# A dilated convolution's last stores: part of them issued by GpSimd, spread anew over the DMA engines

## The chip, the core and the metric

The kernel runs on one core of one Trainium2 chip. The metric is the device time of one launch in microseconds (us); lower is better. Each time is compared with the kernel before as it is printed below.

## What is computed

A 3x3 convolution with dilation 2 and "same" padding: 16 images of 64 channels and 64x64 points, 128 output channels, all in float32 in HBM.

```python
batch, c_in, h, w, c_out, k, dilation = 16, 64, 64, 64, 128, 3, 2
x_pad = np.pad(x, ((0, 0), (0, 0), (4 // 2, 4 // 2), (4 // 2, 4 // 2)))
for b, co, ci, kh, kw:
    output[b, co] += weight[co, ci, kh, kw] * x_pad[b, ci, kh*2:kh*2+h, kw*2:kw*2+w]
```

The input is 16.8 MB, the output 33.6 MB, the weights 0.3 MB.

## The kernel before

**Tiling.** Two images make a pair: 2 x 64 channels fill the 128 partitions, so a pair's input is one tile `x32` of 128 x 4096 float32. There are 8 pairs (`pb`, 0 to 7). A pair's 64 rows are worked on in 4 groups of 16 rows (`g`), so the main loop (L200) runs over G = 0 to 31, with pb = G // 4 and g = G % 4. For each group ScalarE casts input rows to float16 (L74), VectorE adds pairs of rows (L86), TensorE makes three products (`psA`, `psB`, `psP`, all L172), ScalarE copies `psP` to `p_sb` (L234), and VectorE adds `p_sb` to `psA` and to `psB` (L241), which gives the even and the odd pairs of output rows. The two adds write the group's rows into the pair's output tile `osb`: 128 partitions (output channels) x 2 images x 4096 points in float32. Three `osb` tiles are in use in turn.

**Order.** The program is scheduled by hand (`tc.manual_schedule()`, L57): every engine runs its instructions in the order in which they are written, and the framework adds only the waits. All DMAs, loads and stores alike, are issued by SyncE (SP) on one queue. Their completions are told on eight semaphores used in turn, so each DMA of SP waits, before it is issued, until the one eight places ahead of it has landed, besides waiting for the data that it needs. GpSimd (POOL) works only in the first 5.2 us of the program: constants, an identity matrix, and two of the weight transforms (L113, L116).

**How a DMA is cut.** A row of a partition that is contiguous on both sides is one packet. A store of 32 rows of one image over 128 partitions is 128 packets of 8 KB (32 x 64 x 4 bytes); over 16 DMA engines that is 8 packets for each. Each share of a DMA ends with a packet of 4 bytes, which tells the semaphore.

**Stores.** From the fourth pair on (`pb` 3 to 6) a pair is stored when it is finished, one image at a time (L276, L277, 2 MB each). The last pair (`pb` 7, G = 28 to 31) is stored in halves of 32 rows: after G = 29 rows 0 to 32 of image 0 (L269), rows 0 to 24 of image 1 (L271), and rows 24 to 32 of image 1 in two DMAs, one over partitions 0 to 124 and one over partitions 124 to 128 (`FOUR`, L197, L272; `ROWS4 = 8`, L198). After G = 31 rows 32 to 64 of both images follow (L269, L274). The function `store` (L184) makes a DMA of one image, `store_both` (L191) one of both images.

Of the kernel before, what the change touches and what calls it, by code (L numbers as in the profile page):

```python
# [10 lines left out]
def kernel(  # L11
# [7 lines left out]
    nc = tc.nc  # L19

    B, CI, H, W = x.shape
# [7 lines left out]
    P = 128  # L29
    f32 = mybir.dt.float32  # L30
# [5 lines left out]
    GR = 16  # L36
    NG = H // GR
# [7 lines left out]
    wpool = ctx.enter_context(tc.tile_pool(name="wpool", bufs=1))  # L45
# [8 lines left out]
    x_pair = x.rearrange("(nb two) c h w -> nb (two c) (h w)", two=2)  # L54
    out_img = out.rearrange("b o h w -> b o (h w)")
# [3 lines left out]
    x32_tiles, x16_tiles, xs_tiles, o_tiles = {}, {}, {}, {}  # L59

    def load(pb, cuts=(0, H)):
        if pb not in x32_tiles:
            x32_tiles[pb] = fpool.tile([P, HW], f32, tag="x32", name="x32")
        for lo, hi in zip(cuts[:-1], cuts[1:]):
            nc.sync.dma_start(  # L65
                out=x32_tiles[pb][:, lo * W : hi * W], in_=x_pair[pb, :, lo * W : hi * W]
            )
# [10 lines left out]
    def rowsum(c):  # L78
        pb, g = divmod(c, NG)
        if g == 0:  # L80
            xs_tiles[pb] = sxpool.tile([P, HW // 2], f16, tag="xs", name="xs")
        v = x16_tiles[pb][:, g * GR * W : (g + 1) * GR * W].rearrange(
            "p (b e q) -> p b e q", e=2, q=2 * W
        )
        s = xs_tiles[pb][:, g * NH : (g + 1) * NH].rearrange("p (b q) -> p b q", q=2 * W)
        nc.vector.tensor_tensor(out=s, in0=v[:, :, 0], in1=v[:, :, 1], op=add)  # L86
# [27 lines left out]
    nc.scalar.copy(out=wdv[:, 2], in_=wv[:, 0])  # L114
    nc.vector.tensor_tensor(out=wdv[:, 1], in0=wv[:, 2], in1=wv[:, 1], op=sub)
    nc.gpsimd.tensor_copy(out=wdv[:, 4], in_=wv[:, 2])  # L116

    wts = [apool.tile([P, 1024], f32, tag="ab", name="wt") for _ in range(3)]

    def turn(k):  # L120
# [24 lines left out]
        out=x16_tiles[0][:, 8 * W : 18 * W], in_=x32_tiles[0][:, 8 * W : 18 * W]  # L145
# [8 lines left out]
    def casts(G):  # L154
        for n in range(2 if G else 3):
            c = ahead[0]
            if c >= ngroups or c > G + (7 if c < 2 * NG else 5):
                return
            cast(c)
            ahead[0] += 1  # L160

    def product(ps, src, kind, blk0, nblk, first, last):
        for j in (1, 0, 2):
            dw = (j - 1) * d
            o0, o1 = max(0, -dw), W - max(0, dw)
            t = kind * KW + j
            for hb in range(2):
                pp = slice(hb * CI, (hb + 1) * CI)
                rhs = src(pp, dw + o0, dw + o1)
                po = ps[:, hb * NH + blk0 * 2 * W : hb * NH + (blk0 + nblk) * 2 * W]  # L170
                po = po.rearrange("p (r w) -> p r w", w=W)[:, :, o0:o1]
                nc.tensor.matmul(  # L172
                    out=po,
                    lhsT=w_sb[pp, t * CO : (t + 1) * CO],
                    rhs=rhs,
                    start=first and j == 1,
                    stop=last and j == 2,
                )

    def blocks(x16, b0, n, e):  # L180
        v = x16.rearrange("p (b e r w) -> p b e r w", e=2, r=2, w=W)
        return lambda pp, c0, c1: v[pp, b0 : b0 + n, e, :, c0:c1]

    def store(pb, m, r0=0, r1=H, rows=((0, P),)):  # L184
        for lo, hi in rows:
            nc.sync.dma_start(
                out=out_img[2 * pb + m, lo:hi, r0 * W : r1 * W],
                in_=o_tiles[pb][lo:hi, m * HW + r0 * W : m * HW + r1 * W],
            )

    def store_both(pb, r0, r1):  # L191
        nc.sync.dma_start(
            out=out_img[2 * pb : 2 * pb + 2, :, r0 * W : r1 * W].rearrange("m o q -> o m q"),
            in_=o_tiles[pb].rearrange("p (m q) -> p m q", m=2)[:, :, r0 * W : r1 * W],
        )

    FOUR = ((0, P - 4), (P - 4, P))  # L197
    ROWS4 = 8  # L198

    for G in range(ngroups):  # L200
        pb, g = divmod(G, NG)
        x16 = x16_tiles[pb]
        xs = xs_tiles[pb].rearrange("p (r w) -> p r w", w=W)
        if g == 0:
            o_tiles[pb] = opool.tile([P, 2 * HW], f32, tag="osb", name="osb")
        o = o_tiles[pb].rearrange("p (m b e q) -> p m b e q", m=2, e=2, q=2 * W)
        b0 = g * NBLK

        def summed():
            ps = ppool.tile([P, 2 * NH], f32, tag="p", name="psP")  # L210
            sv = lambda pp, c0, c1: xs[pp, g * GR // 2 : (g + 1) * GR // 2, c0:c1]
            product(ps, sv, 0, 0, NBLK, True, True)
            return ps

        if G:
            psP = summed()

        psA = apool.tile([P, 2 * NH], f32, tag="ab", name="psA")
        product(psA, blocks(x16, b0, NBLK, 1), 1, 0, NBLK, True, False)
        z = 1 if g == 0 else 0  # L220
        product(psA, blocks(x16, b0 + z - 1, NBLK - z, 1), 2, z, NBLK - z, False, True)

        psB = apool.tile([P, 2 * NH], f32, tag="ab", name="psB")
        product(psB, blocks(x16, b0, NBLK, 0), 3, 0, NBLK, True, False)
        z = 1 if g == NG - 1 else 0
        product(psB, blocks(x16, b0 + 1, NBLK - z, 0), 4, 0, NBLK - z, False, True)

        if not G:
            psP = summed()

        if not G:
            casts(0)
        p_sb = spool.tile([P, 2 * NH], f32, tag="psb", name="p_sb")
        nc.scalar.copy(out=p_sb, in_=psP)  # L234
        if G:
            casts(G)
        if G + 1 < ngroups:
            rowsum(G + 1)
        pv = p_sb.rearrange("p (m b q) -> p m b q", m=2, q=2 * W)
        for e, ps in ((0, psA), (1, psB)):  # L240
            nc.vector.tensor_tensor(  # L241
                out=o[:, :, b0 : b0 + NBLK, e],
                in0=ps.rearrange("p (m b q) -> p m b q", m=2, q=2 * W),
                in1=pv,
                op=add,
            )

        if G == 0:
            load(XF, (0, H // 2))
        if pb == 0:  # L250
            if g % 2 == 1:
                store_both(0, (g - 1) * GR, (g + 1) * GR)
                if g == 1:
                    load(XF, (H // 2, H))
                else:
                    load(XF + 1)
        elif g == NG - 1 and pb == 1:
            store(1, 0)
            store(1, 1, 0, H // 2)
            load(XF + 2)  # L260
            store(1, 1, H // 2, H)
        elif g == NG - 1 and pb == 2:
            store(2, 0)
            load(XF + 3)
            store(2, 1)
            load(XF + 4)
        elif pb == npairs - 1:
            if g % 2 == 1:
                store(pb, 0, (g - 1) * GR, (g + 1) * GR)  # L269
                if g == 1:  # L270
                    store(pb, 1, 0, 2 * GR - ROWS4)  # L271
                    store(pb, 1, 2 * GR - ROWS4, 2 * GR, FOUR)  # L272
                else:
                    store(pb, 1, (g - 1) * GR, (g + 1) * GR)  # L274
        elif g == NG - 1:
            store(pb, 0)  # L276
            store(pb, 1)  # L277
# [37 lines left out]
```

## Time and profile before

| | us |
|---|---|
| time, median of 3 runs | 126.88 |
| the three runs | 126.70, 127.41, 126.88 |
| span of the profiled execution, first to last instruction | 125.0 |
| what the median has beyond that span | 1.9 |
| busy in the span: TensorE / VectorE / ScalarE / GpSimd | 105.8 / 91.0 / 64.9 / 2.2 |
| time of the SP queue's packets, as a share of 16 DMA engines' span | 96.7% |

The execution that was profiled has no time of its own in the list of runs; its span stands 1.9 us below their median, and this is taken as what lies around it.

How to read it: the page gives each engine's busy time, then the span in 40 slices of 3.1 us (a digit is the busy share in tenths), the DMA queues, and the DMA issues by size. A view by stretches of time gives, for each stretch, the share of the 16 DMA engines' time that packets took (1.00 is all 16 busy; packets are counted where they start, so a stretch can read a little over 1) and the rate in GB/s. The trace also holds every DMA packet with its start, duration and size, but not the number of the engine that moved it. On one engine the packets follow each other without a gap, the next one starting 3 ns before the recorded end of the last, so the records can be joined to 16 chains, one for each engine; where such chains are spoken of below, they were joined in this way.

### The profile page before, as it was taken

What the parts mean: (1) busy time and instruction counts of PE and PEld (TensorE: products, weight loads), DVE (VectorE), ACT (ScalarE), POOL (GpSimd) and SP (SyncE); (2) the same over time, 40 slices, a digit from 0 to 9 for tenths busy, and PEclk for the clock granted to TensorE, in tenths of its full rate; (3) what the DMA queues carried; (4) which work ended last, traced back from release to release, by engine and by line L of the source; (5) the groups of instructions that cost most, each with busy time, mean ns of one, the idle gap of its engine ahead of it and who ended that gap; (6) DMA issues with size and microseconds to landing.
All of it is one profiled execution on the core that took longest, in us unless ns stands there. A gap on an engine that the chain in (4) does not pass through costs nothing.

```text
span 125.0 us, 2343 instructions
## 1 busy us (share of the span) xinstructions
PE 105.8 (85%) x1002; PEld 57.0 (46%) x1002; DVE 91.0 (73%) x103; ACT 64.9 (52%) x68; POOL 2.2 (2%) x8
## 2 busy tenths in 40 slices
PE   6996999999999999999999999999999999600000
PEld 2353555555555555555555555555555555200000
DVE  0561998988898889888988898889888988700000
ACT  4188896665666566656665666566653333100000
POOL 2400000000000000000000000000000000000000
PEclk9999999999999999999999999999999999985555
DMA  5999999999999999999999999999999999999991
GB/s 142 368 450 435 430 401 315 430 422 420 443 427 435 412 441 438 401 435 435 425 430 427 420 435 430 435 420 435 420 430 430 430 425 435 430 414 412 420 395 73
DMA packets 4722, 50.78 MB, mean 406 GB/s; under 512 B 488, under 2 KB 488, under 8 KB 1000
## 3 DMA queue, kind: packets, MB, share of 16 engines
q1 hardware_dynamic: 4712, 50.63, 96.7%
q8 instruction: 8, 0.13, 0.4%
q14 instruction: 2, 0.02, 0.0%
HBM read 17.07 MB, written 33.55 MB: 405 GB/s over the span
## 4 chain that ended last, share of the span: by engine, by line
PE 76%; DMA 6%; ACT 2%; DVE 1%; DVEq 1%; SPq 1%; issue 0%
PE psA L172 31%; PE psB L172 30%; PE psP L172 16%; DMA x<-in_x_dram 6%; ACT x L74 2%; DVE osb L241 1%; DVEq L310 1%; ACT p_sb L234 1%; SPq L65 0%; SPq L89 0%; DVEq L241 0%
## 5 line engine op out<-in xcount | busy, mean ns | idle before, releaser
L172 PEld LDWEIGHTS <-w_sb 64*128 64x128 f16 x960 | 54.6, 94 | 45.8 <-issue 1.4
L234 ACT COPY p_sb<-psP 128x1024 f32<-128x1024 f32 x32 | 32.4, 1012 | 36.9 <-issue 21.5
L241 DVE TENSOR_TENSOR osb<-psA,p_sb 128x1024 f32<-128x1024 f32 x32 | 39.2, 1225 | 13.4 <-PE psA L172 9.8
L172 PE MATMUL psA<-x,w_sb 64*128 64x496 f16 (+3 forms) x384 | 45.1, 365 | 0.0
L172 PE MATMUL psB<-x,w_sb 64*128 64x496 f16 (+3 forms) x384 | 45.1, 365 | 0.0
L241 DVE TENSOR_TENSOR osb<-psB,p_sb 128x1024 f32<-128x1024 f32 x32 | 39.1, 1222 | 0.0
L74 ACT CAST x<-x 128x1024 f16<-128x1024 f32 (+2 forms) x31 | 32.1, 1044 | 0.5 <-DMA x<-in_x_dram 0.3
L172 PE MATMUL psP<-xs,w_sb 64*128 64x496 f16 (+1 forms) x192 | 26.0, 371 | 1.1 <-ACT p_sb L234 1.1
L86 DVE TENSOR_TENSOR xs<-x 128x512 f16<-128x512 f16 x32 | 13.3, 416 | 0.4 <-ACT x L74 0.4
L102 PE MATMUL dm<-zero 128*128 128x512 f16 x12 | 5.3, 579 | 1.2 <-DVE zero L94 1.2
L102 PEld LDWEIGHTS <-zero 128*128 128x128 f16 x12 | 1.4, 128 | 3.2 <-issue 1.8
L112 DVE CAST wd<-w 128x192 f16<-128x192 f32 x1 | 0.5, 503 | 2.4 <-DMA w<-in_weight_dram 2.4
L125 PEld LDWEIGHTS <-wd 128*64 128x64 f16 x30 | 1.0, 118 | 1.8 <-DVE wd L112 0.8
L137 ACT CAST w_sb<-wt 128x384 f16<-128x384 f32 x1 | 0.5, 478 | 2.3 <-PE wt L125 2.3
L114 ACT ACT_TABLE_LOAD x1 | 1.3, 1283 | 0.7 <-PEq L296 0.7
L125 PE MATMUL wt<-ident,wd 128*64 128x128 f16 x30 | 1.6, 241 | 0.0
L114 ACT CAST wd<-w 128x192 f16<-128x192 f32 x1 | 0.5, 539 | 1.5 <-DMA w<-in_weight_dram 1.5
L139 DVE CAST w_sb<-wt 128x384 f16<-128x384 f32 x1 | 0.6, 557 | 0.7 <-PE wt L125 0.7
L135 DVE CAST w_sb<-wt 128x384 f16<-128x384 f32 x1 | 0.6, 558 | 0.5 <-PE wt L125 0.5
L94 DVE MEMSET zero<- 128x256 uint32 x1 | 0.3, 272 | 0.9 <-PEq L296 0.9
L113 POOL TENSOR_TENSOR wd<-w 128x192 f16<-128x192 f32 x1 | 0.8, 799 | 2.3 <-DMA w<-in_weight_dram 2.3
L116 POOL CAST wd<-w 128x192 f16<-128x192 f32 x1 | 0.8, 806 | 0.0
(11 smaller groups left out, 3.8 us busy)
## 6 DMA issues: line engine op xcount, KB each, us to landing
out_dram<-osb SPq DMA_DIRECT2D x13, 2048.0 KB, 14.9
x<-in_x_dram SPq DMA_DIRECT2D x6, 2048.0 KB, 17.0
out_dram<-osb SPq DMA_DIRECT2D x5, 1024.0 KB, 13.1
x<-in_x_dram SPq DMA_DIRECT2D x2, 1024.0 KB, 13.2
x<-in_x_dram SPq DMA_DIRECT2D x1, 1088.0 KB, 5.6
x<-in_x_dram SPq DMA_DIRECT2D x1, 960.0 KB, 7.4
out_dram<-osb SPq DMA_DIRECT2D x1, 768.0 KB, 15.4
w<-in_weight_dram SPq DMA_DIRECT2D x1, 288.0 KB, 2.8
```

Of the source, the lines that this page charges most:

```text
L74: nc.scalar.copy(out=x16_tiles[pb][:, lo * W : hi * W], in_=x32_tiles[pb][:, lo * W : hi * W])
L86: nc.vector.tensor_tensor(out=s, in0=v[:, :, 0], in1=v[:, :, 1], op=add)
L102: nc.tensor.matmul(out=dm[:, 0:512], lhsT=zero[:, 0:P], rhs=zero)
L113: nc.gpsimd.tensor_tensor(out=wdv[:, 3], in0=wv[:, 0], in1=wv[:, 1], op=sub)
L114: nc.scalar.copy(out=wdv[:, 2], in_=wv[:, 0])
L116: nc.gpsimd.tensor_copy(out=wdv[:, 4], in_=wv[:, 2])
L125: nc.tensor.matmul(out=wts[k % 3][r * CI : (r + 1) * CI, c0 + j * CO : c0 + (j + 1) * CO], lhsT=wd[:, t * CI : (t + 1) * CI], rhs=ident,)
L135: nc.vector.tensor_copy(out=t0[0], in_=t0[1])
L172: nc.tensor.matmul(out=po, lhsT=w_sb[pp, t * CO : (t + 1) * CO], rhs=rhs, start=first and j == 1, stop=last and j == 2,)
L234: nc.scalar.copy(out=p_sb, in_=psP)
L241: nc.vector.tensor_tensor(out=o[:, :, b0 : b0 + NBLK, e], in0=ps.rearrange("p (m b q) -> p m b q", m=2, q=2 * W), in1=pv, op=add,)
L310: with _tile.TileContext(nc) as tc:
```

## The change

Three things are changed.

- After the weight transforms GpSimd issues a small load: 5 partitions, two pieces of 16 numbers each, into a new tile `step` that nothing reads.
- After G = 28 GpSimd stores rows 0 to 8 of both images of the last pair over partitions 0 to 121 (`ELEVEN` = 11 x 11), in one DMA with two pieces for each partition. What is left of these rows (partitions 121 to 125, and 125 to 128) is stored by SP after G = 29 in two small DMAs.
- After G = 29 the other stores start at row 8: rows 8 to 32 of image 0, rows 8 to 28 of image 1, and rows 28 to 32 of image 1 in the two DMAs of `FOUR` (`ROWS4` is 4 instead of 8). The stores after G = 31 are the same.

```diff
     nc.gpsimd.tensor_copy(out=wdv[:, 4], in_=wv[:, 2])
+    step = wpool.tile([5, 32], f32, name="step")
+    nc.gpsimd.dma_start(
+        out=step.rearrange("p (s n) -> p s n", s=2),
+        in_=x_pair[0, 0:5, 0 : 2 * W].rearrange("p (s n) -> p s n", s=2)[:, :, 0:16],
+    )
...
-    def store_both(pb, r0, r1):
-        nc.sync.dma_start(
-            out=out_img[2 * pb : 2 * pb + 2, :, r0 * W : r1 * W].rearrange("m o q -> o m q"),
-            in_=o_tiles[pb].rearrange("p (m q) -> p m q", m=2)[:, :, r0 * W : r1 * W],
+    def store_both(pb, r0, r1, lo=0, hi=P, eng=nc.sync):
+        both = out_img[2 * pb : 2 * pb + 2, lo:hi, r0 * W : r1 * W]
+        eng.dma_start(
+            out=both.rearrange("m o q -> o m q"),
+            in_=o_tiles[pb].rearrange("p (m q) -> p m q", m=2)[lo:hi, :, r0 * W : r1 * W],
         )
 
     FOUR = ((0, P - 4), (P - 4, P))
-    ROWS4 = 8
+    ROWS4 = 4
+    ELEVEN = 11 * 11
+    ROWS11 = 8
...
         elif pb == npairs - 1:
-            if g % 2 == 1:
+            if g == 0:
+                store_both(pb, 0, ROWS11, 0, ELEVEN, nc.gpsimd)
+            elif g == 1:
+                store(pb, 0, ROWS11, 2 * GR)
+                store(pb, 1, ROWS11, 2 * GR - ROWS4)
+                store(pb, 1, 2 * GR - ROWS4, 2 * GR, FOUR)
+                store_both(pb, 0, ROWS11, ELEVEN, ELEVEN + 4)
+                store_both(pb, 0, ROWS11, ELEVEN + 4, P)
+            elif g == NG - 1:
                 store(pb, 0, (g - 1) * GR, (g + 1) * GR)
-                if g == 1:
-                    store(pb, 1, 0, 2 * GR - ROWS4)
-                    store(pb, 1, 2 * GR - ROWS4, 2 * GR, FOUR)
-                else:
-                    store(pb, 1, (g - 1) * GR, (g + 1) * GR)
+                store(pb, 1, (g - 1) * GR, (g + 1) * GR)
```

## The prediction, made before the changed kernel ran

> **What bounds the kernel now.** I read the page's slices and queue rows first, to see which resource is full.
>
> ```profile
> DMA  5999999999999999999999999999999999999991
> GB/s 142 368 450 435 430 401 315 430 422 420 443 427 435 412 441 438 401 435 435 425 430 427 420 435 430 435 420 435 420 430 430 430 425 435 430 414 412 420 395 73
> ...
> q1 hardware_dynamic: 4712, 50.63, 96.7%
> ```
>
> The DMA engines are full from the second slice to the last but one, all on SP's queue. So the time is the bytes of each of 16 engines at that engine's rate, and the end is that of the engine that ends last. TensorE and VectorE matter only if a store comes so late that an engine runs dry. The VectorE rows in order of time show when the last groups are written; the waits of SP show what the program's end waits for.
>
> ```profile
> 98.79 1.22 DVE L241 TENSOR_TENSOR osb<-psB,p_sb 128x1024 f32<-128x1024 f32 x1
> ...
> 101.96 1.22 DVE L241 TENSOR_TENSOR osb<-psB,p_sb 128x1024 f32<-128x1024 f32 x1
> ...
> 108.25 1.22 DVE L241 TENSOR_TENSOR osb<-psB,p_sb 128x1024 f32<-128x1024 f32 x1
> ```
>
> ```profile
> SPq L310 <- DMA out_dram<-osb: 13.2, 3, 8.5
> ```
>
> G = 28 is written at 100.0 us, G = 29 at 103.2, G = 31 at 109.5; then nothing but stores runs for 15 us. What counts is how evenly the engines end. The view by stretches shows it:
>
> ```profile
> 119.00:120.00 1.00, 0.00 (x0) 0.00 (x0) 0.00 (x0) 0.00 (x0) 0.00 (x0) 0.50 1.03 434
> 120.00:120.50 0.50, 0.00 (x0) 0.00 (x0) 0.00 (x0) 0.00 (x0) 0.00 (x0) 0.50 0.97 410
> ...
> 121.50:122.00 0.50, 0.00 (x0) 0.00 (x0) 0.00 (x0) 0.00 (x0) 0.00 (x0) 0.50 0.74 311
> 122.00:122.50 0.50, 0.00 (x0) 0.00 (x0) 0.00 (x0) 0.00 (x0) 0.00 (x0) 0.50 0.35 147
> 122.50:123.00 0.50, 0.00 (x0) 0.00 (x0) 0.00 (x0) 0.00 (x0) 0.00 (x0) 0.50 0.31 131
> 123.00:123.50 0.50, 0.00 (x0) 0.00 (x0) 0.00 (x0) 0.00 (x0) 0.00 (x0) 0.50 0.20 82
> 123.50:124.00 0.50, 0.00 (x0) 0.00 (x0) 0.00 (x0) 0.00 (x0) 0.00 (x0) 0.50 0.04 16
> ```
>
> The last column but one, times 16, is the number of busy engines: all until 120.5, about 6 at 122.25, 3 at 123.25. The chains of packets say which. The 2 KB packets of the two `FOUR` stores are on four engines only, 31 + 1 on each; I call these the low four. They end at 122.91, 123.49, 123.68 and 123.81. The twelve others end at 120.35, 120.61, 120.91, eight from 121.73 to 122.61, and one at 123.45. That one is slow: from about 30 us to 108 us its 16 KB packets mostly take some 644 ns, where the others' take 611. So five engines end within 0.9 us, and the mean of all 16 ends is 122.26, which only a perfect spread would reach (1.55 us earlier).
>
> Beside the numbers of engines: 124 rows went to 4 engines, 128 rows go to 16, so an SP transfer is cut into the largest number of equal shares up to 16 that divides its rows.
>
> **The change, part by part.** Packet prices from the chains, start to start: 8 KB 306 ns, 6 KB 230, 2 KB 80 (84 recorded). A line through 80 and 306 gives 193 for 5 KB and 42 for 1 KB.
>
> 1. Rows 0 to 8 leave the two wide stores after G = 29. Every engine saves 8 x (306 - 230) = 0.61 us on image 0. On image 1 the wide part shrinks from 24 to 20 rows: 8 x (230 - 193) = 0.30. Together -0.91 on all 16.
>
> 2. `FOUR` with half the rows: on the low four 32 x 80 = 2.56 becomes 32 x 42 = 1.34. The two small SP stores (4 and 3 rows, two pieces of 2 KB) put 2 x 80 = 0.16 each on the low four and on three of them. Net for the low four: -0.91 - 2.56 + 1.34 + 0.32 = -1.81 (-1.97 for one). They end at 122.0 at the latest and no longer set the end.
>
> 3. The GpSimd store: 121 rows. By the same division that is 11 engines with 11 rows, 22 packets of 2 KB. No row shows a packet of GpSimd's queue. From below, the nearest row is SP's 2 KB store packet, 80 ns; nothing makes it cheaper, since the bytes are the same. From above, I take the only second queue in the trace, the instruction fetch of 16 KB: it cost its engine 1.33 us where a data packet costs 0.607, 2.2 times, so 176 ns. I take 84, the recorded duration without the overlap of 3 to 4 ns, because it is the same kind of transfer (SBUF to HBM, 2 KB) and packets of two queues need not overlap. So 22 x 84 = 1.85, and with part 1 +0.94 on eleven engines (up to 22 x 176 = 3.87, +2.96).
>
> 4. Which eleven? The load over 5 rows goes ahead of the store, on 5 engines. If GpSimd's transfers go round the engines from the lowest, the store lies on numbers 5 to 15, and number 4 gets only part 1, -0.91. The trace doesn't number the twelve; I assume that the slow one is one of the eleven, which by count alone is 11 in 12. It then ends at 123.45 + 0.94 = 124.39, against 123.81 now: **+0.58**. The next is 122.61 + 0.94 = 123.55.
>
> By the Trainium skill ("DMA: Bandwidth & Descriptors", "Latency and other measured facts") engines 7 and 15 are usually the slow ones, which it ties to descriptor rings of GpSimd's path. The trace agrees that one engine is slow (644 ns against 611), though before the change no DMA is on that path, so the reason given can't be this one. By that rule the slow engine has a number from 5 to 15 and the sum is the one above; without it the count 11 in 12 stands.
>
> 5. The small load: 10 packets of 64 bytes at about 6 us, on five engines. They can't cost more than the weight load's 2304-byte packets (mostly 93 ns): two for each engine, under 0.2 us on engines that don't end last. On GpSimd it comes behind its last transform (ends at 5.1 us), with nothing after it until G = 28. Zero.
>
> 6. Issue and waits. GpSimd waits for VectorE's G = 28 (100.0 us) and then writes the descriptors. The data are wanted by about 117 us only, since each engine has SP's stores queued until then: zero unless that takes over 10 us. SP issues six DMAs after G = 29 instead of four, 0.73 us each, from 103.2 to 107.6, ahead of G = 31 (109.5): zero. But the last pair now has eight SP DMAs instead of six, so by the turn of eight semaphores the two last stores wait for the two stores of pair 6, which landed at 109.86 and 114.73, plus what GpSimd's packets push them back (up to 1.85). The first may be issued at up to 111.5 instead of 109.5, the second at about 116.6 instead of 109.9. With 0.7 us of issue and 0.6 to the first packet (the weight load: issued 0.74, first packet 1.76) the second is there at 117.9. The first low engine that wants it ends its share of the first at 122.91 - 1.81 - 2.45 = 118.65. So 0.75 us of cover: zero. If the cover went (176 ns per packet: landing at 118.6, packets at 119.9) the low four would idle 1.25 us and end by 123.2, still not last.
>
> 7. The program's end waits for each semaphore in turn. Now the last store's is the last; after the change it comes earlier in that row, and GpSimd's two are added. I put 0.15 us, two or three passed waits at the 0.06 us between the last waits of the trace; bounds 0 and 0.4.
>
> Sum: +0.58 + 0.15 = +0.73. Against the profiled execution: 125.0 + 0.7 = 125.7 us of span; with the 1.9 between this span and the median of 126.88: **127.6 us**.
>
> **Rivals.**
>
> *The slow engine is the spared one (number 4).* Not slower. It then gains 0.91 and ends at 122.54; the end is the next of the eleven, 123.55, -0.26 against 123.81, with 0.15 for the waits 126.8. It decides as soon as the engine at 123.45 is outside the eleven. If in the timed runs it lags more than here, the time before is later by as much and the time after isn't: 1.0 us of further lag gives 125.8. For it: it is the only engine that the change relieves relative to the eleven, and the trace has no numbers. Against it: one in twelve by count.
>
> *GpSimd's packets cost more.* At 176 ns the slow engine ends at 123.45 + 2.96 = 126.4, +2.6, with the waits 129.6; halfway, at 130 ns, 128.6. For it: the fetch rows, where a switch between queues cost about 0.7 us beyond the packet itself. Against it: a fetch isn't a store from SBUF.
>
> *The eleven are other engines, or sixteen.* If the store starts at the lowest engine as SP's do, the low four get 1.85 as well and end at 123.81 - 1.81 + 1.85 = 123.85: 127.1 if the slow engine isn't hit, 127.6 if it is. If the rows go to 16 engines, 8 rows each, an engine takes 16 x 84 = 1.34 and nets +0.43: the slow one ends at 123.88, 127.1; were it the one with a single row left, 126.5. For the last the skill (same page, "Why a DMA increments its semaphore by 16 and not by 1") knows a spread by 16 for some GpSimd copies and going round in turn for the others; no row here shows either.
>
> **How the numbers follow.** Forecast (slow engine among the eleven, packets of 80 to 100 ns, waits 0 to 0.4: 127.3 to 128.2): 0.40. Slow engine spared (125.8 to 127.0): 0.30; more than the count gives, because the twelve aren't numbered and the same time comes out if that engine is slow only while it is recorded. Dearer packets (128.2 to 129.6): 0.20. Other engines (126.5 to 127.6): 0.10. The bound for a change is 0.5%, 0.63 us, about what separates the three runs. Over 127.5: 0.30 of the forecast and all of the dearer packets, 0.50. Under 126.25: 0.17 of the spared, 0.03 of the last. The rest 0.30. The range 126.1 to 129.2 leaves out some 0.10 below and 0.08 above; the forecast's own is 127.3 to 128.2.
>
> **What would show it.** A second data queue with 252 data packets; 22 packets of 2 KB from it on each of eleven chains, at about 84 ns; the low four ending about 122; a share of 16 engines that stays near 1 until 121.2 and a single engine left after 123.6. I am wrong if the last engine is one of the many, or if all engines idle before the last store.

## The result, and the profile after

The changed kernel takes 128.80 us (median of four runs, 128.55 to 129.13) against 126.88 for the three runs of the kernel before; the ratio is 1.0155, with a 95% interval of 1.0114 to 1.0196. A fourth run of before (130.27) was disturbed and isn't in the ratio. The forecast was 127.6, with a range of 126.1 to 129.2. The profiled execution took 129.13, with a span of 127.3, so 1.85 us lie around it.

The lines below are from the page of the changed kernel: the slices and the queues.

```profile
DMA  4999999999999999999999999999999999999970
GB/s 130 380 458 438 417 404 366 440 391 422 448 438 422 404 456 389 435 420 427 438 420 422 417 427 433 438 407 443 422 438 417 433 427 404 415 383 367 385 296 41
...
q1 hardware_dynamic: 4733, 50.13, 94.9%
q0 software_dynamic: 224, 0.50, 1.0%
```

Still no empty slice before the end, and the second queue (q0, GpSimd's) has only 0.50 MB. Its 224 packets are, for the store, 121 of 4 KB, 55 of 8 bytes and 16 of 4 bytes, and for the load 5 of 128 bytes, 11 of 8 and 16 of 4. So the 4 KB packets lie on 11 engines, 11 on each, and every engine outside gets 8-byte packets in their place, 11 on each of five; I call these padding. But the slices 36 to 38 carry 383, 367 and 385 GB/s, where the kernel before had 414, 412 and 420: the engines are busy and move less. The view by stretches of the same kernel shows where (the last two columns are the DMA share and the rate):

```profile
104.00:106.00 2.00, 2.00 (x23) 1.01 (x19) 1.62 (x2) 0.10 (x1) 0.00 (x0) 1.00 0.95 403
106.00:108.00 2.00, 2.00 (x22) 1.11 (x20) 1.25 (x2) 1.01 (x1) 0.00 (x0) 1.00 0.98 393
108.00:110.00 2.00, 0.56 (x8) 0.13 (x3) 1.91 (x2) 0.00 (x0) 0.00 (x0) 1.00 1.05 418
110.00:112.00 2.00, 0.00 (x0) 0.00 (x0) 0.00 (x0) 0.00 (x0) 0.00 (x0) 1.00 0.99 397
...
116.00:118.00 2.00, 0.00 (x0) 0.00 (x0) 0.00 (x0) 0.00 (x0) 0.00 (x0) 0.50 0.99 313
118.00:119.00 1.00, 0.00 (x0) 0.00 (x0) 0.00 (x0) 0.00 (x0) 0.00 (x0) 0.50 0.95 339
...
124.00:125.00 1.00, 0.00 (x0) 0.00 (x0) 0.00 (x0) 0.00 (x0) 0.00 (x0) 0.50 0.25 107
```

The same stretches of the kernel before, which the prediction didn't show:

```profile
104.00:106.00 2.00, 2.00 (x24) 1.05 (x20) 2.00 (x2) 0.19 (x1) 0.00 (x0) 1.00 1.03 442
106.00:108.00 2.00, 2.00 (x22) 1.00 (x18) 1.25 (x2) 0.82 (x1) 0.00 (x0) 1.00 0.99 418
108.00:110.00 2.00, 0.11 (x2) 0.00 (x0) 1.46 (x2) 0.00 (x0) 0.00 (x0) 1.00 1.05 442
110.00:112.00 2.00, 0.00 (x0) 0.00 (x0) 0.00 (x0) 0.00 (x0) 0.00 (x0) 0.92 0.91 389
...
116.00:118.00 2.00, 0.00 (x0) 0.00 (x0) 0.00 (x0) 0.00 (x0) 0.00 (x0) 0.50 1.03 426
118.00:119.00 1.00, 0.00 (x0) 0.00 (x0) 0.00 (x0) 0.00 (x0) 0.00 (x0) 0.50 1.05 436
...
124.00:125.00 1.00, 0.00 (x0) 0.00 (x0) 0.00 (x0) 0.00 (x0) 0.00 (x0) 0.50 0.00 0
```

Two stretches lose bytes while the share stays near 1. From 116 to 119 us the kernel before moves 2 x 426 + 436 = 1288 KB, the changed one 2 x 313 + 339 = 965. At some 27 KB per us and engine (16 KB in 0.607 us), 323 KB over 16 engines are 0.75 us of every engine. From 104 to 112 us it is 3382 against 3222 KB, 0.37 us. A share near 1 with a low rate means packets that take longer than their size. The packet records say the same. Take for every packet its recorded time beyond the normal one of its size (611 ns for 16 KB, 309 for 8 KB, 234, 196, 159, 84 and 46 for 6, 5, 4, 2 and 1 KB); from 97 us on this sums to 0.08 us per engine before and to 1.08 after. I call it stall. There are two bursts: 16 KB packets, from 106 to 112 us, while GpSimd's store runs; and the small and 8 KB packets after that, mostly from 116 to 119 us, when GpSimd's store has landed (112.5 to 114.9 us).

SP's queue and the waits, in the changed kernel (first the DMA issues in order of time: start, duration; then waits: total, times, longest):

```profile
103.66 6.16 SPq L191 DMA_DIRECT2D out_dram<-osb  x4
109.87 3.15 SPq L198 DMA_DIRECT2D out_dram<-osb  x2
113.11 4.68 SPq L191 DMA_DIRECT2D out_dram<-osb  x2
```

```profile
SPq L322 <- DMA out_dram<-osb: 8.3, 1, 8.3
...
SPq L191 <- DMA out_dram<-osb: 3.3, 1, 3.3
```

Before, four issues after G = 29 took 0.33, 0.64, 0.73 and 0.73 us. Now six take 0.33, 1.66, 1.97, 2.05, 1.68 and 1.42, so the first store of G = 31 is issued at 113.11 instead of 109.49. The last is issued at 117.44, after the wait of 3.3 us for the landing of a store of pair 6 (117.43). VectorE is only 0.45 us later than before (the last writes of G = 28, 29 and 31):

```profile
99.24 1.23 DVE L249 TENSOR_TENSOR osb<-psB,p_sb 128x1024 f32<-128x1024 f32 x1
...
102.41 1.23 DVE L249 TENSOR_TENSOR osb<-psB,p_sb 128x1024 f32<-128x1024 f32 x1
...
108.69 1.21 DVE L249 TENSOR_TENSOR osb<-psB,p_sb 128x1024 f32<-128x1024 f32 x1
```

Where the 2.3 us of span went can be read from the landings, 16 for each wide store. I measure from the mean landing of the store of pair 5's second image (issued at about 85 us, ahead of everything that the GpSimd store touches; 102.97 before, 103.09 after) to the mean landing of the last store, and call this the drain.

| | before | after | difference |
|---|---|---|---|
| mean landing of pair 5's second image | 102.97 | 103.09 | +0.12 |
| from there to the mean landing of the last store (drain) | 19.64 | 20.87 | +1.23 |
| from that mean to the last landing | 1.53 | 2.12 | +0.59 |
| from the last landing to the end of the span | 0.86 | 1.23 | +0.37 |

So over half is time that the average engine lost, not imbalance. The bytes are the same in both kernels; 1.00 of the 1.23 is stall.

### The profile page after: what moved, and what is told of

Its sections match the earlier page's. It is cut to its first block, busy times and chain, and to the rows that moved or that the text cites. A ratio compares the mean times of both kernels' runs of the same rounds, so it can differ in the third digit from the quotient of the medians.

```text
span 127.3 us, 2348 instructions
## 1 busy us (share of the span) xinstructions
PE 106.2 (83%) x1002; PEld 56.5 (44%) x1002; DVE 90.8 (71%) x103; ACT 64.8 (51%) x68; POOL 3.7 (3%) x10
## 4 chain that ended last, share of the span: by engine, by line
PE 82%; ACT 2%; DVE 1%; DVEq 1%; issue 1%
PE psA L177 31%; PE psB L177 30%; PE psP L177 16%; PE dm L102 4%; DVE osb L249 1%; DVEq L322 1%; ACT p_sb L242 1%; PE wt L130 1%; ACT x L152 0%; ACT w_sb L153 0%; DVE zero L94 0%; ACT w_sb L142 0%; DVEq L249 0%
## 5 line engine op out<-in xcount | busy, mean ns | idle before, releaser
L177 PEld LDWEIGHTS <-w_sb 64*128 64x128 f16 x960 | 53.9, 94 | 46.5 <-issue 1.4
L198 POOL DMA_DIRECT2D out_dram<-osb x1 | 0.8, 832 | 94.8 <-DVE osb L249 94.8
```

What stands on the lines that cost most here:

```text
L177: nc.tensor.matmul(out=po, lhsT=w_sb[pp, t * CO : (t + 1) * CO], rhs=rhs, start=first and j == 1, stop=last and j == 2,)
L198: eng.dma_start(out=both.rearrange("m o q -> o m q"), in_=o_tiles[pb].rearrange("p (m q) -> p m q", m=2)[lo:hi, :, r0 * W : r1 * W],)
```

## Experiments

The theory after reading the traces: the GpSimd store over 121 partitions lies on 11 engines, the other five get the padding, and while or after this runs SP's packets stall. Rivals: the small load, the smaller rows of `FOUR`, the small SP stores (and with them the turn of the eight semaphores), or any GpSimd store. All kernels below are cut from the kernel before or from the changed one. The table has, for the profiled execution of each, the mean duration of SP's issues that follow another directly after G = 29, the stall of the 16 KB and 4 KB packets, the stall of the smaller and 8 KB packets (us per engine, from 97 us on), and the drain; then the ratio to the kernel before in the timed runs.

| kernel | GpSimd load / store | SP issue | stall 16, 4 KB | stall others | drain | ratio (95%) |
|---|---|---|---|---|---|---|
| before | none | 0.70 | 0.08 | 0.00 | 19.64 | 1 |
| `rows4` | none | 0.62 | 0.08 | 0.00 | 19.65 | 1.0009 (0.9983 to 1.0035) |
| `step_only` | load / none | 1.14 | 0.08 | 0.01 | 19.67 | 1.0032 (1.0012 to 1.0052) |
| `sp_cut` | none | 1.64 | 0.08 | 0.00 | 19.72 | 1.0019 (1.0001 to 1.0038) |
| `gp128` | none / 16 engines | 0.76 | 0.08 | 0.00 | 19.68 | 1.0036 (1.0010 to 1.0062) |
| `gp128_sp8` | none / 16 engines | 0.63 | 0.09 | 0.00 | 19.69 | 1.0020 (0.9980 to 1.0061) |
| `gp128_step` | load / 16 engines | 1.21 | 0.08 | 0.17 | 19.96 | 1.0056 (1.0027 to 1.0086) |
| `after_nostep` | none / 11 engines | 1.32 | 0.12 | 0.41 | 20.22 | 1.0106 (1.0061 to 1.0151) |
| `no_left` | load / 11 engines | 1.93 | 0.49 | 0.69 | 20.94 | 1.0153 (1.0126 to 1.0181) |
| changed kernel | load / 11 engines | 1.76 | 0.40 | 0.68 | 20.87 | 1.0155 (1.0114 to 1.0196) |
| `after_again` | load / 11 engines | 1.83 | 0.53 | 0.74 | 21.03 | 1.0200 (1.0157 to 1.0243) |

**Only the smaller rows of FOUR** (on the kernel before).

```diff
-    ROWS4 = 8
+    ROWS4 = 4
```

> The kernel before with ROWS4 = 4 instead of 8, and nothing else: the wide part of image 1 is 28 rows (7 KB packets) and the two FOUR stores have packets of 1 KB. Theory 'placement' (what counts is how many bytes each engine gets): the low four lose 1.22 us and every engine gains 0.3, so the end goes from a low engine (123.8) to the slow one at 123.45 + 0.3: no change, ratio 0.997 to 1.002. Theory 'small rows' (packets of 1 KB, and rows that start at odd multiples of 1 KB, stall all engines): packets of 6 to 8 KB with 50 to 500 ns too much from about 115 us on, as in the changed kernel, and 0.5 to 1 us more, ratio 1.004 to 1.008.

Measured: 126.99 us, ratio 1.0009, no stalls. The small packets are harmless by themselves. The low four now end about 1 us earlier (by the chains the latest at 122.83, before 123.81) and the time doesn't move, because the slow engine is now the last, at 123.65 (before 123.45).

**Only the small load** (on the kernel before).

```diff
     nc.gpsimd.tensor_copy(out=wdv[:, 4], in_=wv[:, 2])
+    step = wpool.tile([5, 32], f32, name="step")
+    nc.gpsimd.dma_start(
+        out=step.rearrange("p (s n) -> p s n", s=2),
+        in_=x_pair[0, 0:5, 0 : 2 * W].rearrange("p (s n) -> p s n", s=2)[:, :, 0:16],
+    )
```

> The kernel before plus the small GpSimd load, which nothing reads. All theories but one: no change, ratio 0.998 to 1.002. Theory 'start': if the load itself disturbs the first 10 us (the changed kernel's first store was issued at 17.4 us, before at 16.95) or leaves engines further apart, the first store comes at 17.4 again and the four last engines are 2 us behind the others at 105 us; then up to 1.005.

Measured: 127.44 us, ratio 1.0032: a small loss of 0.4 us, which the theories hadn't: the only one with a loss tied it to a first store at 17.4 us, and that was issued at 16.94. The load has landed by 11.0 us, and yet 90 us later SP's issues still take 1.14 to 1.19 us instead of 0.64 to 0.73. With the load alone nothing waits for that. There are no stalls, and the queue of SP in order of time shows the same six issues in a stretch 0.5 us longer than the 7.35 of before.

```profile
103.20 7.87 SPq L192 DMA_DIRECT2D out_dram<-osb  x6
```

**The changed kernel's cut, all by SP.** Rows 0 to 8 are stored by SP over all 128 partitions after G = 28; no load, no small stores.

```diff
-                store_both(pb, 0, ROWS11, 0, ELEVEN, nc.gpsimd)
+                store_both(pb, 0, ROWS11)
...
-                store_both(pb, 0, ROWS11, ELEVEN, ELEVEN + 4)
-                store_both(pb, 0, ROWS11, ELEVEN + 4, P)
```

> The changed kernel's cut of the rows, but rows 0 to 8 of both images are stored by SP over all 128 partitions after G = 28: no GpSimd DMA, no small load, no leftover stores. Every engine gets 16 packets of 2 KB (1.28 us) there and saves 0.91; the low four lose 0.85 net. Theory 'placement': low four end at 122.96, the slow one at 123.8, no change, ratio 0.998 to 1.003. Theory 'small rows': the stalls after 115 us stay, 1.004 to 1.01. Theory 'GpSimd queue' (the second queue stalls all engines and slows SP's issues): the stalls and the SP issues of 1.4 to 2.0 us are gone, SP issues take 0.7 us again, no change in time.

Measured: 127.06 us, ratio 1.0019, no stalls. Cutting the rows so costs next to nothing.

**The same store by GpSimd over 16 engines.** As the last, but issued by GpSimd.

```diff
-                store_both(pb, 0, ROWS11, 0, ELEVEN, nc.gpsimd)
+                store_both(pb, 0, ROWS11, 0, P, nc.gpsimd)
...
-                store_both(pb, 0, ROWS11, ELEVEN, ELEVEN + 4)
-                store_both(pb, 0, ROWS11, ELEVEN + 4, P)
```

> As the changed kernel, but the GpSimd store covers all 128 partitions (16 engines alike), without the small load and the leftover stores. Theory 'placement' (the eleven were the wrong engines): every engine gets the same 8 packets of 4 KB (1.25 us), so no change against before, ratio 0.998 to 1.004. Theory 'GpSimd queue': packets of other sizes are stalled while it runs (50 to 500 ns too much on many 16 KB packets, 0.3 us for each engine) and after 116 us, SP issues take 1.4 to 2 us, and the time is 1 to 1.5 us over before, ratio 1.008 to 1.013.

Measured: 127.38 us, ratio 1.0036. A GpSimd store beside SP's is not what stalls: its 128 packets of 4 KB alternate with SP's 16 KB packets, and the rates by stretches of this kernel stay whole (3406 KB from 104 to 112 us, 1277 from 116 to 119).

```profile
104.00:106.00 2.00, 2.00 (x23) 1.03 (x19) 2.00 (x2) 0.39 (x1) 0.00 (x0) 1.00 0.93 395
106.00:108.00 2.00, 1.91 (x20) 0.89 (x16) 1.25 (x2) 0.62 (x1) 0.00 (x0) 1.00 1.06 442
108.00:110.00 2.00, 0.00 (x0) 0.00 (x0) 1.26 (x2) 0.00 (x0) 0.00 (x0) 1.00 0.96 403
110.00:112.00 2.00, 0.00 (x0) 0.00 (x0) 0.00 (x0) 0.00 (x0) 0.00 (x0) 0.80 1.09 463
...
116.00:118.00 2.00, 0.00 (x0) 0.00 (x0) 0.00 (x0) 0.00 (x0) 0.00 (x0) 0.50 1.04 422
118.00:119.00 1.00, 0.00 (x0) 0.00 (x0) 0.00 (x0) 0.00 (x0) 0.00 (x0) 0.50 1.03 433
```

**The changed kernel again, unaltered.**

> The changed kernel once more, unaltered, beside the next one and with more rounds. Ratio 1.01 to 1.02 as measured first. If the slow packets from 106 to 122 us (about 1 us for each engine) belong to the change, they are in this trace too, and SP's issues after G = 29 take 1.4 to 2.0 us again; if they were an accident of one execution, neither is there and some 1.5% is left unexplained by them.

Measured: 129.80 us (128.66 to 130.84), ratio 1.0200 (1.0157 to 1.0243), with both bursts again: the stalls are no accident of one profile.

**The changed kernel without the small load.** The six lines of the load are left out.

> The changed kernel without the small GpSimd load. Theory 'the load turns the engines' (GpSimd's transfers go round the 16 engines): each launch now starts 11 further on, so the eleven differ from launch to launch and the times of one kernel spread over 1 us or more (126.5 to 129). Theory 'always from the lowest engine': every launch as the others, the low four carry both, and the time is that of the changed kernel, within 0.3%. Theory 'the load costs by itself' (0.3%, as the load alone did): 0.4 us less than the changed kernel.

Measured: 127.96 us, ratio 1.0106. Without the load the first burst is all but gone (0.12 against 0.08 of the kernel before) and the second is smaller, 0.41. By the chains the store now begins at the lowest engine: the low four and the slow engine carry 11 packets of 4 KB each, and the padding lies on five of the others. That is the placement of the theory 'always from the lowest engine', but neither its time (that of the changed kernel) nor that of 'the load costs by itself' (0.4 us less) came: it is 1.8 us less than the changed kernel beside it. Whether the start moves from launch to launch, one trace can't show; the six times lie between 127.72 and 129.52. From 116 to 119 us this kernel moves 2 x 337 + 422 = 1096 KB, 192 fewer than the kernel before, 0.44 us per engine:

```profile
116.00:118.00 2.00, 0.00 (x0) 0.00 (x0) 0.00 (x0) 0.00 (x0) 0.00 (x0) 0.50 0.98 337
118.00:119.00 1.00, 0.00 (x0) 0.00 (x0) 0.00 (x0) 0.00 (x0) 0.00 (x0) 0.50 1.04 422
```

**Numbering the engines.** In both kernels the last row of the last store is cut into DMAs of 5, 7, 8, 12, 15 and 81 partitions. Since an SP transfer goes to the largest number of engines up to 16 that divides its rows, the one of 5 lands on five, right behind these engines' share of the wide store.

```diff
-                    store(pb, 1, (g - 1) * GR, (g + 1) * GR)
+                    store(pb, 1, (g - 1) * GR, H - 1)
+                    store(pb, 1, H - 1, H, ((0, 5), (5, 12), (12, 20), (20, 32), (32, 47), (47, P)))
```

> The kernel before, with the last row of the last store cut into six DMAs of 5, 7, 8, 12, 15 and 81 partitions. By the division rule these lie on the 5, 7, 8, 12, 15 and 9 lowest engines, so the last packets of each chain tell which engine it is (0-3 by FOUR, 4, 5-6, 7, 8, 9-11, 12-14, 15). Forecast of the prediction: the slow engine (16 KB packets of 644 ns) is one of 5 to 15. Rival 'spared': it is 4. The time is up to 1 us longer by the added DMAs.

> The changed kernel with the same cut of the last row. Forecast: GpSimd's 4 KB packets lie on the engines 5 to 15, 11 each, and the low four and engine 4 have none. Rival 'other engines': the low four, which alone have packets of 1 KB, carry them too; then they end 1.75 us later than forecast, at 122.9 to 123.9. The time is up to 1 us longer than the changed kernel's.

Measured, one execution each: 127.99 and 129.37 us. In the kernel before, the DMA of 5 landed at 123.20, 123.38, 123.83, 124.00 and 124.26, each 0.17 to 0.19 behind a landing of the wide store at 123.02, 123.20, 123.66, 123.81 and 124.08. Four of these are the low four: the small `FOUR` store landed on them at 118.30, 118.47, 118.94 and 119.35, and two shares of 2.35 us lead from there to 123.00, 123.17, 123.64 and 124.05. The fifth, 123.81, is the slow engine: the 6 KB store's last landing, 118.93, leads by 2.45 us for each 8 KB store to 121.38 and 123.81. So **the slow engine is number 4**. Joined also by the order in which the packet sizes of the stores must come, the chains say the same of the changed kernel, of the numbered one and of `no_left` below: the padding lies on the four chains with the 1 KB packets and on the slow one, and the 4 KB packets on the eleven others. So the forecast of the engines 5 to 15 held, and the rival 'other engines' falls. In the numbered changed kernel the DMA of 5 landed at 123.60, 123.86, 124.02, 124.15 and 125.68, so its five lowest engines ended their wide share at 123.44, 123.69, 123.84, 123.98 and 125.52. The other eleven ended theirs from 121.84 to 125.37.

**Sixteen engines, eight SP stores.** `gp128` with `FOUR` cut finer, so that the last pair again has eight SP stores and the last one waits for pair 6.

```diff
-    FOUR = ((0, P - 4), (P - 4, P))
+    FOUR = ((0, P - 4), (P - 4, P - 2), (P - 2, P - 1), (P - 1, P))
```

> As the run with GpSimd's store over all 128 partitions (16 engines, ratio 1.0036, no stalls), but the four rows of partition 124 to 128 go out in three small SP stores (2, 1 and 1 partitions) instead of one, so that the last pair again has eight SP stores and the last one waits for pair 6. Theory A (the eleven engines and the padding on the other five are the cause, the late last store is harmless): ratio 1.002 to 1.006, stalls under 0.2 us per engine, although the last store is issued at about 117. Theory B (the small SP stores and the turn of the semaphores make the second burst, at 116 to 119 us): a burst of 0.4 to 0.7 us per engine there, ratio 1.008 to 1.011.

Measured: 127.49 us, ratio 1.0020, no stalls; the last store was issued at 116.01, after SP had waited for pair 6 (8.2 us in two waits):

```profile
SPq L185 <- DMA out_dram<-osb: 8.2, 2, 4.6
```

Theory B falls: small SP stores and a last store issued 6 us later cost nothing that can be seen.

**Eleven engines, six SP stores.** The changed kernel without its two small SP stores (rows 0 to 8 of partitions 121 to 128 are left out).

```diff
-                store_both(pb, 0, ROWS11, ELEVEN, ELEVEN + 4)
-                store_both(pb, 0, ROWS11, ELEVEN + 4, P)
```

> The changed kernel without the two small SP stores: rows 0 to 8 of partitions 121 to 128 are not written. The last pair has six SP stores, so the last store doesn't wait for pair 6 and is issued by about 112. Theory A (the eleven engines and the padding are the cause): stalls near 1 us per engine stay, ratio 1.011 to 1.019 (0.03 us per engine less to move). Theory B: the first burst (106 to 112 us, 0.3 to 0.45) stays, the second (116 to 119, 0.6 to 0.7) goes, ratio 1.005 to 1.010.

Measured: 128.91 us, ratio 1.0153, as theory A had it (1.011 to 1.019). Both bursts stay, though no store waits for pair 6. The rate of this kernel falls in the same stretches:

```profile
110.00:112.00 2.00, 0.00 (x0) 0.00 (x0) 0.00 (x0) 0.00 (x0) 0.00 (x0) 1.00 0.95 375
...
116.00:118.00 2.00, 0.00 (x0) 0.00 (x0) 0.00 (x0) 0.00 (x0) 0.00 (x0) 0.50 0.94 290
118.00:119.00 1.00, 0.00 (x0) 0.00 (x0) 0.00 (x0) 0.00 (x0) 0.00 (x0) 0.50 0.98 367
```

And SP needs 10 us for the six issues, none of it waiting, where `gp128` needed 7.4 with a wait of 3.4 in them (first `no_left`, then `gp128`):

```profile
103.66 9.99 SPq L191 DMA_DIRECT2D out_dram<-osb  x6
```

```profile
103.01 7.44 SPq L186 DMA_DIRECT2D out_dram<-osb  x6
```

**The small load ahead of a store over 16 engines.** The changed kernel with `gp128`'s store, and the load kept.

> The small load over 5 partitions and GpSimd's store over all 128 (16 engines, 8 packets of 4 KB each), no small SP stores. If the small load does harm by itself (alone it gave 1.0032), its cost adds to the store's 1.0036: ratio 1.006 to 1.008, SP's issues 1.0 to 1.2 us. If it does harm only because it turns the store to engines 5 to 15, ratio 1.002 to 1.005. If, with a load ahead of it, a store over 16 engines stalls too (the cause is a store that begins at engine 5, or the load, not the padding on five engines): stalls over 0.5 us per engine and 1.010 or more.

Measured: 127.85 us, ratio 1.0056 (1.0027 to 1.0086), between the two first cases; of the third (0.5 us and 1.010) only a trace: no first burst, but 0.14 of the 0.17 us per engine of stall is in the 1 KB packets, which are on the low four alone (by the chains 1.1 us on each of two of them, under 0.1 on the others). The rate from 116 to 119 us of this kernel:

```profile
116.00:118.00 2.00, 0.00 (x0) 0.00 (x0) 0.00 (x0) 0.00 (x0) 0.00 (x0) 0.50 0.97 379
118.00:119.00 1.00, 0.00 (x0) 0.00 (x0) 0.00 (x0) 0.00 (x0) 0.00 (x0) 0.50 1.03 399
```

**One row instead of eight on the eleven engines.** The changed kernel with a GpSimd store of row 0 alone (rows 1 to 8 of its 121 partitions are left out).

```diff
-                store_both(pb, 0, ROWS11, 0, ELEVEN, nc.gpsimd)
+                store_both(pb, 0, 1, 0, ELEVEN, nc.gpsimd)
```

> The changed kernel with a GpSimd store of row 0 alone over the 121 partitions: rows 1 to 8 of these are not written, so each of the eleven engines has 1.5 us less to move than in the changed kernel, the other five have the same padding packets and packets to switch between. If the stalls come from the number of GpSimd's packets between SP's and the padding beside them: stalls in the first burst as in the changed kernel, 0.3 to 0.45 us per engine, and most of the second. If they come from the bytes that GpSimd's store moves: an eighth of that, under 0.1 us per engine. Time: the most loaded engines end 0.9 us earlier than in the kernel before, the low four by 1.8; without stalls the slow engine and the low four end near 122.5, 125.6 us in all (ratio 0.990); with stalls of 1 us 126.6 to 127.0 (0.998 to 1.001).

Measured: 126.92 us, ratio 0.9988 (0.9959 to 1.0017). The question wasn't answered as put, because the packets didn't stay the same: on each of the eleven engines the 22 rows of 256 bytes went as two packets, 4096 and 1536 bytes, and on the other five the padding as two packets of 64 and 24 bytes, that is 11 times 8. With two packets instead of eleven there is no first burst, and of the second 0.21 us per engine. So the first burst isn't due to the presence of a store on 11 engines; it needs many packets of it, or its bytes. The time fell short of the forecast of 125.6 by more than the stalls: 434 KB less should drain 1.0 us sooner, it was 0.72 (18.92), and the profiled execution was already 0.6 us late at the start of that stretch (103.59), with the last landing there 3.0 us behind the mean instead of 1.8.

**What the runs settle, and what stays open.** Shown: the loss needs the store on 11 engines. `no_left` and `gp128_step`, measured side by side, differ by nothing but the rows of GpSimd's store, 121 or 128: 1.0153 against 1.0056. In all four comparisons that have the store on 11 engines in full the ratio is 1.0106 to 1.0200, with the same rows on 16 it is 1.0020 to 1.0056. The load ahead of the store makes the loss larger; the small SP stores, the turn of the semaphores and the row cut don't matter.

Where the first burst lies can be read from the chains. In the changed kernel, `no_left` and the numbered changed kernel, 62 of the 120 SP packets of 16 KB that stand beside padding on the low four (from 104.5 to 114 us) take over 60 ns too long; on engine 4, which has the same padding, none of 33; beside 4 KB packets on the other eleven 7 of 343. Without the load the padding lies on five other engines, and there it is 3 of 54; with 4 KB packets on all 16 (`gp128`) it is 1 of 121. So in these runs the first burst comes only where many padding packets lie on the low four, and padding alone doesn't make it. What the load does to this burst is to put the padding there. The low four are also the engines to which SP sends the `FOUR` stores at that time; whether that is the other half of the cause wasn't tried (the changed kernel without `FOUR`).

The second burst is on nearly every engine of the changed kernel. Without the load 0.35 of its 0.41 us is on the five engines that had the padding, though GpSimd's last packet there started at 114.35 and the burst begins at 115.5. It goes with SP's issue time: none at 0.6 to 0.8 us, 0.17 to 0.21 at about 1.2 with a GpSimd store, 0.41 at 1.32, 0.68 to 0.74 at 1.8 and more. That this is cause and effect isn't shown: no kernel changed the issue time alone, `step_only` has 1.14 without stalls, and the mean of `sp_cut` is one issue of 3.42 us, again without stalls. Why the load lengthens SP's issues for the rest of the program, and what the padding does to the packets beside it and after it, stays open. A kernel with padding but without GpSimd data wasn't tried. No version was faster than the kernel before.

## Why the prediction was right about the direction, and where it failed

The time lay in the range and on the side that was likeliest, 1.2 us above the number. But the working got there on a wrong reason for the loss. That the time still lay in the range is luck: the engine that was to set the end was spared, and a loss that the sum didn't have took its place.

*(1) Shorter wide stores.* Right: 5 KB packets took 196 ns, 6 KB 234, 1 KB 46, close to the line (193 and 230 to 234, 42).

*(2) Low four end by 122.0.* Failed. By the chains they ended at 123.20, 123.49, 124.23 and 125.35, which is 1.2 to 3.4 us too late. The step's prices were right, and the stalls are what it left out: 1.0 to 1.2 us in the first burst alone on each of the four. One of them is again among the last; the very last, at 125.73, is one of the eleven.

*(3) GpSimd's packets.* The price was right, the form wasn't: the two pieces of 2 KB go as one packet of 4 KB, 121 in all, 159 ns each (79.5 per 2 KB; forecast 84). So 11 x 159 = 1.75 us on eleven engines, where 1.85 was forecast. The rival with dearer packets (130 to 176 ns) falls by its own mechanism, though its time, 128.6, is the nearest to what was measured: what became dearer are SP's packets, beside the padding and after GpSimd's store. The upper row, the 16 KB fetch, was the right warning on the wrong packet.

*(4) Which eleven.* The step that failed first. It assumed that the slow engine is one of the eleven, 11 in 12 by count. It is number 4, and the store lies on 5 to 15, so it is spared (it ended at 123.29) and the +0.58 that carried the forecast doesn't exist. The rival "spared" (0.30) had this right and gave 126.8; it is wrong by 2.0 us, because it holds only if nothing else is lost. The records carry no engine numbers; that the eleven are 5 to 15 follows from the padding, which lies on the low four and on the slow engine. The Trainium skill ("DMA: Bandwidth & Descriptors", "Why a DMA increments its semaphore by 16 and not by 1") has GpSimd's transfers on k engines in a row from a cursor that goes round, with k the largest number up to 16 that divides the rows. With 121 data packets and 55 padding packets, 11 on each of five engines, the trace agrees on k = 11. On the cursor two traces agree with it: with the load over 5 rows ahead the store begins behind the five lowest engines, and without it (`after_nostep`) at the lowest. The rule that engines 7 and 15 are usually the slow ones (same page, "Latency and other measured facts") isn't borne out: the slow one here is number 4, at 644 against 611 ns, and it was slow before GpSimd issued any DMA.

*(5) The small load costs nothing.* Wrong: alone 0.4 us (1.0032), and with the store on 11 engines the difference between 1.0106 and 1.0200, measured side by side. The step counted its packets on the engines, rightly as nothing, and didn't ask whether it changes SP's issues (1.14 us instead of 0.70) or what the engines that it spares get. No row of the trace of before could have shown that.

*(6) Issue and waits.* The working used 0.73 us for an issue; with 1.4 to 2.0 the first store of G = 31 came at 113.1 (bound 111.5; by its own terms, 109.86 + 1.85, it should have been 111.7) and the last at 117.4 (116.6). The conclusion, zero, held: `gp128_sp8` issues its last store at 116.0 and loses nothing, and the changed kernel's share stays at 0.99 from 116 to 118 us.

*(7) End waits.* 0.15 forecast; after the last landing six waits pass, 0.06 us apart, from 126.09 to 126.41, and the end of the program comes 0.37 us later after that landing than before. Inside the bounds 0 to 0.4.

What was missing is a term that none of the seven steps nor a rival had: stalls of SP's own packets, 1.00 us for the mean engine. Parts 1 to 4 leave the mean of the 16 ends 0.13 later; the drain came out 1.23 longer. "I am wrong if the last engine is one of the many" was the test that caught it: the last engine is one of the eleven and not the slow one, and from 124 to 125 us the share is still 0.25, four engines, where one was forecast after 123.6.

## What to carry to other kernels

Where DMA is the bound, balancing engines by hand gains at most the spread of their ends (here 1.55 us), so find out first which engine is the slow one; a DMA over 5 rows at the end, landing on the lowest five, shows in one run whether it is among these. A share near 1 doesn't say that bytes move: read the rate beside it, stretch by stretch. And don't put a GpSimd transfer over fewer than 16 engines beside a full SP queue without measuring it: here nearly the same bytes cost 0.2 to 0.4% over all 16 engines and 1.1% over 11, and with a small GpSimd load ahead 0.6% and 1.5 to 2.0%.

## What the runs showed of the hardware

- A GpSimd store over 11 engines sends the other five 11 packets of 8 bytes each; SP's 16 KB packets beside these took up to 1.24 us instead of 0.61 on engines 0 to 3 of the changed kernel, and no longer than usual on engine 4.
- GpSimd's queue packs short rows into packets of up to 4 KB: two of 2 KB at 159 ns; 22 of 256 bytes as 4096 + 1536; two of 64 bytes as one of 128.
- A GpSimd load of 640 bytes at 5 us makes SP's issues longer from about 85 us to the end of the program (1.14 us instead of 0.70 after G = 29); a store on 11 engines does too (1.32), and both together give 1.8 to 1.9.
- From the end of GpSimd's issue to its first packet it takes 3.2 us (load: 5.23 + 0.70, first packet at 9.1) to 3.9 us (store: 100.77 + 0.83, first packet at 105.47). Here it was hidden.
- In the kernel before an instruction fetch of 16 KB cost its engine about 1.33 us: 0.97 recorded at 95.1 us, and the packet behind it took 0.99 instead of 0.61. The last four of the eight fetches fell on four different engines.
